# Three more matmul steps by seven products in a fused attention and MLP layer: pair 6 of two output groups, pair 1 of one down pass

## The chip, the cores and the metric

The kernel runs on one core of a Trainium2 chip. The metric is the device time of one execution in microseconds (us), as the median of several runs. The profile is one execution, recorded by the hardware profiler.

## The reference

One layer of a streaming encoder on 256 tokens (T) with width 2048 (D), all in float32, and a final norm. The part that matters here:

```python
h = x
h = h + _gla_mixer(_rmsnorm(h, gla_norm), w_in, ..., w_out)   # ends in (o * silu(r)) @ w_out
h = h + _sq_relu_mlp(_rmsnorm(h, mlp_norm), w_up, w_down)     # relu(h @ w_up)**2 @ w_down, hidden width 8192
return _rmsnorm(h, final_norm)
```

`w_out` is 2048 x 2048, `w_up` 2048 x 8192, `w_down` 8192 x 2048. Each weight is read once from HBM.

## The kernel before, in words

**Precision.** TensorE multiplies in a shortened float32 form (fp32r). A float32 product is made of three: high part by high part, high by low, low by high. So each weight tile goes through three steps after its load lands in a `raw` buffer: ScalarE casts it (`copy_hi`, L123: `hi<-raw`), VectorE subtracts (L136: `lo<-raw,hi`), and then TensorE multiplies, 256 columns at a time.

**A step by sums.** The code takes weights in pairs of channel tiles (`kp`: two tiles of 128 rows by 512 columns). A plain step over a pair takes 24 matmuls of 256 columns. A step by sums treats the pair as a 2 x 2 block product and makes it of seven block products in place of eight (a Strassen-like scheme), so 21 matmuls. They come in two halves. The first half (9 matmuls) uses three of the four blocks as they are. For the second half (12 matmuls, issued one step later, called `pending` in the code), the blocks are replaced by sums of blocks. Beside the matmuls, a step by sums differs from a plain one in this:

- The load comes as two halves of 256 KB (L334 in the output groups) in place of one of 512 KB (L337).
- POOL sends one more DMA that adds a block from HBM on top of the raw tile (L335, `accum_op=ALU.add`, 128 KB; in the down passes L1233). It must follow the first half's landing. SyncE sends all plain loads.
- ScalarE casts 768 columns for the first half, and 512 + 512 of the sums for the second (all L123).
- VectorE makes the low part of the 768 columns (L136), the weight sums L233 (256 columns, which waits for the accumulate) and L234 (512), and later the low part of the sums (1024: L365 in the output groups, L1293 in the down passes).
- The raw buffer is held until that last low part. For a plain step it is free after L136.
- The products go to four accumulators: two that hold the result blocks (B32 and BX4 in the down passes), and two that hold mixed products (P16 and P57), which are folded in at the end of a group.

On the activation side such a pair needs its tile in eight forms rather than four (sums of its blocks, `form_sums`).

**The raw buffers.** There are six (`raw_tile`, a tile pool). A new tile gets the buffer that is released first in the program's order, and its load waits for the release. The loads go out on SyncE's queue in order, so a load that waits holds back those behind it.

**The output groups** (`out_group`, `group`). `w_out` is taken in four groups of 512 columns, each over all eight pairs. The later three use the order of pairs 1, 3, 7, 2, 0, 6, 4, 5 (`ORDER[1]`). By sums are pairs 0, 1, 6, 7 in the first and the fourth group, 0, 1, 7 in the second and third. Four steps ((1, 1), (2, 1), (3, 1) and (3, 6) as group and pair) have their sums made earlier and read back from HBM. At the end of a group, `combine` folds the mixed products (two copies on ScalarE, then L926 to L929 on VectorE), and `put` (L934, one for each half of the tokens) adds that to the accumulators and writes the group's 512 columns of `h`. In the next group, after its third step (pair 7), `turn` transposes those columns on TensorE (L845), scales them (ScalarE L858, VectorE L859), for use as input to the MLP.

**The MLP** (`up`, `down`). Eight rounds m of 1024 hidden channels. Up steps and down steps alternate, step by step; the up steps run ahead, so that the end of the last rounds' down passes runs without any up step between. A pass (m, g) multiplies the round's four pairs (kp 0 to 3) of `w_down` into output group g. A fresh pass gets its accumulators one by one: `begin` copies the saved content of an accumulator into a free PSUM bank (ScalarE L1150), after `settle` has copied the last pass's content of that accumulator home and freed its bank. Mixed accumulators are begun where the first step by sums of the pass is (`first`). The last round has only passes (7, 0) and (7, 1) in this form; the second half of the columns of this round is done in the last stage by rows of `w_down` (L181), followed by the final norm. In the last round, pairs 2 and 3 of pass (7, 0) and pair 2 of pass (7, 1) are by sums.

**The order of instructions** is set by a scheduler on top of the program's order, with constraints (`issue_after`) that keep casts and low parts of the weights in sequence.

Of the kernel before, what the change touches and what calls it, by code (L numbers as in the profile page):

```python
# [69 lines left out]
def tile_gla_mlp(ctx, tc, x, xt, cols, w_vg, w_in, w_gate, w_out, w_up, w_down, final_norm, out):  # L70
# [755 lines left out]
    FORMED = (0, 1, 6, 7)  # L826
# [12 lines left out]
    def turn(src, row, gain, q, forms_of=None, banks=None):  # L839

        bs = banks or [aux_bank(), aux_bank()]
        for i in range(4):
            kt, b, o = 4 * q + i, bs[i // 2], i % 2 * T
            for t in range(NT):
                newest[0] = nc.tensor.matmul(  # L845
                    b[:, o + t * P : o + (t + 1) * P], src[:, t, kt * P : (kt + 1) * P], ident, is_transpose=True,
                    start=i % 2 == t == 0, stop=i % 2 == t == 1, skip_group_check=True,
                ).ins
        for kp in (2 * q, 2 * q + 1):
            if forms_of and kp in FORMED:  # L850
                turn_pair(kp, bs[kp - 2 * q], gain, forms_of(kp))
                continue
            for kt in (2 * kp, 2 * kp + 1):
                i = kt - 4 * q
                b, o = bs[i // 2], i % 2 * T
                s = b[:, o : o + T].rearrange("p (t s) -> p t s", t=NT)
                dh, dl = row(kt)
                nc.scalar.activation(dh, s, AF.Copy, scale=gain(kt))  # L858
                nc.vector.scalar_tensor_tensor(dl, s, gain(kt), dh.bitcast(F32), op0=ALU.mult, op1=ALU.subtract)  # L859
# [7 lines left out]
    def forms_o(kp):  # L867
        if kp < 2:
            return [of_pairs[:, kp, i] for i in range(2)]
        c = (12 * T + OFF + 128, OFF)[kp - 6]  # L870
        return [in_forms(a[:, c : c + G]) for a in (oth, otl)]
# [24 lines left out]
    def begin_out(g):  # L896

        for t in range(NT):
            out_banks[g, t] = bank = psum_bank(out_ids[2 * (g % 2) + t])
            nc.scalar.copy(bank, h[:, t, g * GT : (g + 1) * GT])  # L900
# [19 lines left out]
    def out_group(g, order, summed, between):  # L920

        def combine(p16, p57):
            tt = nc.vector.tensor_tensor
            nc.scalar.copy(comb[:, 1:3], two(p16))
            nc.scalar.copy(comb[:, 0:4:3], two(p57))
            tt(comb[:, 2], comb[:, 1], comb[:, 2], op=ALU.add)  # L926
            tt(comb[:, 0], comb[:, 0], comb[:, 2], op=ALU.subtract)
            tt(comb[:, 4], comb[:, 0], comb[:, 3], op=ALU.subtract)
            tt(comb[:, 5], comb[:, 2], comb[:, 3], op=ALU.add)  # L929

        def put(banks):
            for t in range(NT):
                o = h[:, t, g * GT : (g + 1) * GT].rearrange("p (f s) -> p f s", f=2)
                nc.vector.tensor_tensor(o, two(banks[t]), comb[:, 4 * t : 4 * t + 2], op=ALU.add)  # L934

        def at_of(kp):
            f = forms_o(kp)
            return lambda k: [a[:, k] for a in f]

        group(  # L940
            lambda kp: w_out[2 * kp * P : 2 * (kp + 1) * P, g * GT : (g + 1) * GT], [out_banks[g, t] for t in range(NT)], out_ids[4:],
            order, summed, between, row_o, at_of, combine, put, ready_of=lambda kp: made.get((None, g, kp)),
        )

    def ssq_h(g):
        for t in range(NT):
            sq = tmp.tile([P, GT], F32, tag="t512", name="sq", bufs=1)
            nc.scalar.activation(sq, h[:, t, g * GT : (g + 1) * GT], AF.Square, accum_out=hs[:, t, g : g + 1])

    ORDER = (3, 0, 2, 1, 4, 7, 6, 5), (1, 3, 7, 2, 0, 6, 4, 5)  # L950
# [6 lines left out]
    hth, htl = (big.tile([P, KT, T], F32R, tag="A" + i, name="h" + i, bufs=1) for i in "hl")  # L957
    turned_h = lambda kt: [a[:, kt, :].rearrange("p (t s) -> p t s", t=NT) for a in (hth, htl)]
    for g in range(1, GROUPS):
        out_group(g, ORDER[1], FORMED if g == 3 else (0, 1, 7), {  # L960
            2: lambda: turn(h, turned_h, g2, g - 1), 4: lambda: ssq_h(g - 1),
            **({3: lambda: begin_out(g + 1)} if g + 1 < GROUPS else {}),
        })
# [38 lines left out]
    def order_of(m):  # L1002

        return range(GROUPS)[:: 1 if m % 2 else -1]

    def by_sums(m, g, kp):

        if m == ROUNDS - 1:
            return (g, kp) in ((0, 2), (0, 3), (1, 2))
        return m < ROUNDS - 2 or g != order_of(m)[-1] or kp in (1, 2)  # L1010


# [105 lines left out]

    form = form.rearrange("p (f s) -> p f s", f=8)
    ways_of = lambda m, kp: {by_sums(m, g, kp) for g in range(GROUPS)}  # L1120

    def forms(m, kp, s):
# [64 lines left out]
    def down(passes):  # L1187
# [7 lines left out]
        for n, (m, g) in enumerate(passes):  # L1195
            fresh = not n or passes[n - 1][1] != g
            if fresh:
# [3 lines left out]
                if m == ROUNDS - 1:  # L1201
                    flush()
            ends = n + 1 == len(passes) or passes[n + 1][1] != g
            first = min(kp for kp in range(KP) if by_sums(m, g, kp)) if fresh else None

            if fresh:
                quick = first == 0
            for kp in range(KP):
                last = ends and kp == KP - 1
                alone = units + LEAD >= UPS  # L1210
                by_parts = by_sums(m, g, kp)

                def products(n, these, w, banks=banks, last=last):
# [261 lines left out]
```

## Time and profile before

| | us |
|---|---|
| median of 3 runs | 1039.96 |
| lowest, highest | 1039.46, 1041.04 |
| profiled execution | 1040.18 |
| its span, first to last instruction | 1038.4 |

| Engine | busy, us | instructions |
|---|---|---|
| TensorE (PE) | 1030.1 | 9013 |
| VectorE (DVE) | 907.3 | 1260 |
| ScalarE (ACT) | 756.0 | 1134 |
| POOL | 136.2 | 182 |

How to read the views. A row of the timeline has a start (us from the span's start), a duration, the engine, the line in the kernel, the operation, `out<-in` by the program's names, the shapes, and a count where several follow one another. What stands in brackets is idle time of the engine before the row and what ended it. `PE` is TensorE, `DVE` VectorE, `ACT` ScalarE, `SPq` SyncE's queue of DMAs. A row of a group view has the count, then the busy time and the mean duration in ns, then idle time and its releasers. A row of DMA issues has the count, the size of one, and the time from its issue to its landing in us. A row of the windows has the stretch, the sum of busy time, TensorE's busy time with its matmuls, the granted clock as a share of the full clock, the DMA share and GB/s.

### The profile page before, as it was taken

Reading aid. Unit: us, or ns where it says so; the run is one execution under the profiler, and the core shown is the slowest. Engines: PE = TensorE matmul, PEld = TensorE weight load, DVE = VectorE, ACT = ScalarE, POOL = GpSimd, SP = SyncE. Lnnn points to the kernel's source line nnn. Section 1 sums busy time; section 2 is a strip of 40 time slices with the busy share of each in tenths; the row PEclk is TensorE's granted clock in tenths of the full one; section 3 lists DMA queues with packets and bytes.
Section 4 is the critical chain, followed back from the end, with each engine's and each line's share of the span. In section 5 each row is a group of like instructions: output and inputs, shape, how many; then the busy total and the mean of one; then the engine's idle time right before and its main releaser. Section 6 shows DMA issues by size and latency. Waiting matters only on the chain.

```text
span 1038.4 us, 23392 instructions
## 1 busy us (share of the span) xinstructions
PE 1030.1 (99%) x9013; PEld 1029.5 (99%) x9013; DVE 907.3 (87%) x1260; ACT 756.0 (73%) x1134; POOL 136.2 (13%) x182
## 2 busy tenths in 40 slices
PE   9999999999999999999999999999999999999997
PEld 9999999999999999999999999999999999999997
DVE  7769769898698776989999999999999999999987
ACT  7775556676477665678779788778788778878785
POOL 0000101310100001111111111111111111111100
PEclk9999999999999999999999999999999999999999
DMA  9967868858878787678888888887888888887872
GB/s 343 332 191 212 268 186 236 211 152 308 255 230 257 242 259 198 184 208 238 231 238 228 229 235 228 236 237 224 247 228 220 250 228 229 235 237 216 239 242 91
DMA packets 128911, 240.30 MB, mean 231 GB/s; under 512 B 11504, under 2 KB 30320, under 8 KB 128672
## 3 DMA queue, kind: packets, MB, share of 16 engines
q1 hardware_dynamic: 107488, 215.32, 65.6%
q0 software_dynamic: 20592, 21.90, 12.4%
q8 instruction: 70, 1.15, 0.4%
q10 hardware_dynamic: 720, 1.60, 0.4%
q14 instruction: 41, 0.34, 0.1%
HBM read 232.48 MB, written 6.29 MB: 230 GB/s over the span
## 4 chain that ended last, share of the span: by engine, by line
PE 97%; DMA 1%; issue 1%; DVE 1%; ACT 0%; POOL 0%; POOLq 0%; DVEq 0%
PE up L1023 34%; PE acc L1023 28%; PE acc L305 15%; PE acc L181 10%; PE acc L224 6%; PE aux L224 2%; PE aux L845 1%; PE aux L696 1%; PE aux L181 1%; DMA raw<-in_w_in 0%; DMA colt<-in_cols 0%; ACT hi L123 0%; ACT sqf L1362 0%; DVE lo L136 0%; DVE comb L745 0%
## 5 line engine op out<-in xcount | busy, mean ns | idle before, releaser
L123 ACT CAST hi<-raw 128x512 fp32r<-128x512 f32 (+4 forms) x658 | 519.8, 820 | 197.9 <-DVE raw L233 66.1
L136 DVE TENSOR_TENSOR lo<-raw,hi 128x768 fp32r<-128x768 f32 (+4 forms) x228 | 233.0, 1031 | 52.9 <-ACT hi L123 49.0
L1023 PE MATMUL acc<-hi,act 128*128 128x256 f32 x1694 | 247.6, 276 | 0.0
L1023 PE MATMUL up<-hh,hi 128*128 128x256 f32 x1024 | 238.7, 276 | 0.0
L1023 PE MATMUL up<-hl,hi 128*128 128x256 f32 x1024 | 238.7, 276 | 0.0
L1023 PEld LDWEIGHTS acc<-hi,act 128*128 128x128 f32 x1694 | 217.4, 188 | 0.0
L170 DVE TENSOR_TENSOR lo<-raw,hi 128x1024 fp32r<-128x1024 f32 x160 | 194.5, 1219 | 21.5 <-ACT hi L123 18.6
L1023 PEld LDWEIGHTS up<-hl,hi 128*128 128x128 f32 x1024 | 192.3, 188 | 0.0
L1023 PEld LDWEIGHTS up<-hh,hi 128*128 128x128 f32 x1024 | 192.3, 188 | 0.0
L1233 POOL DMA_DIRECT2D raw<-in_w_down x113 | 96.9, 857 | 517.3 <-DMA raw<-in_w_down 263.2
L1293 DVE TENSOR_TENSOR lo<-raw,hi 128x1024 fp32r<-128x1024 f32 x113 | 137.7, 1218 | 1.1 <-ACT hi L123 1.1
L1023 PE MATMUL up<-hh,lo 128*128 128x256 f32 x1024 | 137.0, 276 | 0.0
L1023 PE MATMUL acc<-lo,act 128*128 128x256 f32 x847 | 133.9, 276 | 0.0
L1023 PEld LDWEIGHTS up<-hh,lo 128*128 128x128 f32 x1024 | 125.7, 188 | 0.0
L1023 PEld LDWEIGHTS acc<-lo,act 128*128 128x128 f32 x847 | 113.3, 188 | 0.0
L234 DVE TENSOR_TENSOR raw<-raw 128x512 f32<-128x512 f32 x139 | 95.9, 690 | 3.4
L233 DVE TENSOR_TENSOR raw<-raw 128x256 f32<-128x256 f32 x139 | 58.7, 423 | 11.6 <-DMA raw<-in_w_out 8.1
L181 PE MATMUL acc<-hi,xA 128*128 128x256 f32 (+1 forms) x376 | 55.6, 280 | 0.4 <-ACT hi L123 0.4
L181 PEld LDWEIGHTS acc<-hi,xA 128*128 128x128 f32 x376 | 49.5, 189 | 0.7 <-ACT hi L123 0.7
L224 PE MATMUL acc<-xA,hi 128*128 128x256 f32 x288 | 49.2, 276 | 0.0
L1150 ACT COPY sums<-acc 128x512 f32<-128x512 f32 x46 | 26.9, 585 | 22.8 <-PE acc L1023 22.7
L224 PEld LDWEIGHTS acc<-xA,hi 128*128 128x128 f32 x288 | 43.3, 188 | 0.0
(226 smaller groups left out, 1445.8 us busy)
## 6 DMA issues: line engine op xcount, KB each, us to landing
raw<-in_w_up SPq DMA_DIRECT2D x128, 512.0 KB, 4.6
raw<-in_w_down SPq DMA_DIRECT2D x226, 256.0 KB, 4.4
raw<-in_w_in SPq DMA_DIRECT2D x68, 512.0 KB, 4.9
raw<-in_w_down POOLq DMA_DIRECT2D x113, 128.0 KB, 5.1
raw<-in_w_out SPq DMA_DIRECT2D x22, 512.0 KB, 6.6
raw<-in_w_down SPq DMA_DIRECT2D x15, 512.0 KB, 5.5
raw<-in_w_vg SPq DMA_DIRECT2D x14, 520.0 KB, 8.4
raw<-in_w_in SPq DMA_DIRECT2D x24, 256.0 KB, 5.0
```

The source lines that it names most:

```text
L123: last_hi[0] = nc.scalar.copy(to, raw)
L136: last_lo[0] = nc.vector.tensor_tensor(lo[:, s], raw[:, s], hi[:, s].bitcast(F32), op=ALU.subtract)
L170: last_lo[0] = nc.vector.tensor_tensor(to[1], dst, to[0].bitcast(F32), op=ALU.subtract)
L181: newest[0] = nc.tensor.matmul(o[:, m], x, w[:, m], start=first and c == 0, stop=last, skip_group_check=True).ins
L224: nc.tensor.matmul(o, u[:, i, s], m, start=kt == 0 and n == 0 and j % 2 == 0, stop=kt == KT - 1 and n == 2, skip_group_check=True,)
L233: nc.vector.tensor_tensor(u[:, 2], u[:, 0], u[:, 2], op=ALU.subtract)
L234: return nc.vector.tensor_tensor(u[:, 1::2], u[:, 1::2], u[:, 2:3].to_broadcast([P, 2, T]), op=ALU.subtract)
L305: newest[0] = nc.tensor.matmul(bank[:, o + d : o + d + T], x, w[:, d : d + T], start=(not filled or bank in sums_banks) and bank.name not ...
L1023: newest[0] = nc.tensor.matmul(o, x, w, start=first, stop=last, skip_group_check=True).ins
L1150: last_end[0] = nc.scalar.copy(to, src).ins
L1233: nc.gpsimd.dma_start(out=raw[:, :T], in_=src[:, 0, T:], accum_op=ALU.add)
L1293: last_lo[0] = nc.vector.tensor_tensor(to[1][:, :G], u, to[0][:, :G].bitcast(F32), op=ALU.subtract)
```

## The change

Pair 6 goes by sums in the second and third output group (g = 1 and 2) too, and pair 1 of the pass (7, 1) as well.

```diff
     for g in range(1, GROUPS):
-        out_group(g, ORDER[1], FORMED if g == 3 else (0, 1, 7), {
+        out_group(g, ORDER[1], FORMED, {
             2: lambda: turn(h, turned_h, g2, g - 1), 4: lambda: ssq_h(g - 1),
...
     def by_sums(m, g, kp):
 
         if m == ROUNDS - 1:
-            return (g, kp) in ((0, 2), (0, 3), (1, 2))
+            return (g, kp) in ((0, 2), (0, 3), (1, 1), (1, 2))
         return m < ROUNDS - 2 or g != order_of(m)[-1] or kp in (1, 2)
```

`FORMED` is (0, 1, 6, 7). The eight forms of the activations for pair 6 are made before already, since the first and fourth group use them. Those of the last round's pair 1 are new: three VectorE instructions (`form_sums`), and a cast (L1135) and a low part (L1136) of 1024 columns in place of 512. In the pass (7, 1) `first` becomes 1. POOL sends three accumulates more, 12 in place of 10 for `w_out` and 114 in place of 113 for `w_down`.

As a pair by sums holds its raw buffer longer, the buffers are handed on in another order. Pair 7 of the third group had the buffer of the second group's pair 6, free after its L136; now it has that of pair 0, free after its L365. Pair 2 of the third group now has that of pair 4, and pair 0 that of pair 6 (after its L365). In the fourth group pair 7 has the buffer of the third group's pair 7 (after its L365; before, that of pair 6 after its L136).

The last combine of a group now follows the second half of pair 6 rather than that of pair 0.

On VectorE, around the end of the second output group and the third group's first steps. Here L136 of 768 columns and L233, L234 belong to pair 7 of the third group; L926 to L929 and L934 end the second group. Before:

```order
L136 TENSOR_TENSOR lo<-raw,hi 128x768
L926 TENSOR_TENSOR some<-some 128x256
L233 TENSOR_TENSOR raw<-raw 128x256
L927 TENSOR_TENSOR some<-some 128x256
L929 TENSOR_TENSOR some<-some 128x256
L234 TENSOR_TENSOR raw<-raw 128x2x256
L928 TENSOR_TENSOR some<-some 128x256
L136 TENSOR_TENSOR lo<-raw,hi 128x1024
L934 TENSOR_TENSOR h<-acc,some 128x512 x2
L365 TENSOR_TENSOR lo<-raw,hi 128x1024
```

And now:

```order
L136 TENSOR_TENSOR lo<-raw,hi 128x768
L233 TENSOR_TENSOR raw<-raw 128x256
L136 TENSOR_TENSOR lo<-raw,hi 128x1024
L234 TENSOR_TENSOR raw<-raw 128x2x256
L926 TENSOR_TENSOR some<-some 128x256
L927 TENSOR_TENSOR some<-some 128x256
L929 TENSOR_TENSOR some<-some 128x256
L365 TENSOR_TENSOR lo<-raw,hi 128x1024
L928 TENSOR_TENSOR some<-some 128x256
L934 TENSOR_TENSOR h<-acc,some 128x512
L136 TENSOR_TENSOR lo<-raw,hi 128x768
L934 TENSOR_TENSOR h<-acc,some 128x512
```

All four combines stand behind L233 now, and the L365 of pair 7 stands ahead of both L934, with the 768 columns of pair 0 between them.

On ScalarE, in the pass (7, 1), the difference of the two orders. The first two L1150 take P16 home and bring it back for this pass, the next two P57.

```order
-L123 CAST hi<-raw 128x1024
-L123 CAST hi<-raw 128x768
-L1150 COPY sums<-acc 128x512
-L1150 COPY acc<-sums 128x512
-L123 CAST hi<-raw 128x1024
+L123 CAST hi<-raw 128x768
+L1150 COPY sums<-acc 128x512
+L1150 COPY acc<-sums 128x512
+L123 CAST hi<-raw 128x768
+L1150 COPY sums<-acc 128x2x256
+L1150 COPY acc<-sums 128x512
+L123 CAST hi<-raw 128x2x256 x2
```

Before, the casts of pairs 1 and 2 stood ahead of P16's copies, and pair 3's cast between P16 and P57. Now P16 follows pair 1's cast at once, pair 2's cast stands between the copies, and the casts of pair 1's sums follow P57.

## The prediction

> **What bounds the kernel now.** I read the page first: engines, clock, chain.
>
> ```profile
> PE 1030.1 (99%) x9013; PEld 1029.5 (99%) x9013; DVE 907.3 (87%) x1260; ACT 756.0 (73%) x1134; POOL 136.2 (13%) x182
> ...
> PEclk9999999999999999999999999999999999999999
> ...
> PE 97%; DMA 1%; issue 1%; DVE 1%; ACT 0%; POOL 0%; POOLq 0%; DVEq 0%
> ```
>
> TensorE is busy 99% of the span and makes 97% of the chain, at a full granted clock. So a matmul removed is worth its pitch, and any wait that TensorE doesn't have now is paid in full. The timeline and the windows by engine give the pitch, the one pause near the change, and what followed it (start, duration, what; for the windows, TensorE's busy time and matmuls).
>
> ```profile
> 301.61 1.22 DVE L136 TENSOR_TENSOR lo<-raw,hi 128x1024 fp32r<-128x1024 f32 x1
> 302.97 0.41 PE L305 MATMUL acc<-lo,oth 128*128 128x256 f32 x2
> 304.00:312.00 8.00, 8.00 (x70) 1.00 1.01 299
> 318.00:326.00 8.00, 8.00 (x73) 1.00 0.82 267
> ```
>
> A low part came about 20 ns late (301.61 + 1.22 = 302.83) at 302.97. Afterwards 8 us held 70 matmuls, though the window is full; later, past the transposes at 313.12, they held 73. Some two of each count are cut by the window's edges, so that is about 118 ns a matmul against 113: TensorE keeps a slower pace after a pause until a specially laid step (the odd-placed tile `kp in even`, or the transposes) comes by. I take 0.1134 us for one matmul, and 4.1% for the slow pace.
>
> **The change part by part.** I sum against the profiled execution (1040.18: span 1038.4 and 1.8 around it), which stands 0.22 above the median 1039.96 of the runs. Each new step by sums drops 3 of 24 matmuls: 3 x 3 x 0.1134 = **1.02 us less**, 0.34 a step. That is the whole gain. The costs lie in three places.
>
> *Second and third output group.* The rows are VectorE's order, TensorE's transposes of a finished group (L845), SyncE's loads, and the times from a load's or an accumulate's issue to its landing (the last two rows are POOL's accumulates by the group code, of the output groups and of the whole kernel).
>
> ```profile
> 312.44 0.68 DVE L934 TENSOR_TENSOR h<-acc,some 128x512 f32<-128x512 f32 x1
> 313.12 1.03 PE L845 MATMUL aux<-ident,h 128*128 128x128 f32 x8
> 317.74 1.22 DVE L365 TENSOR_TENSOR lo<-raw,hi 128x1024 fp32r<-128x1024 f32 x1
> 318.87 3.22 DVE L136 TENSOR_TENSOR lo<-raw,hi 128x1024 fp32r<-128x1024 f32 x3
> 322.79 0.62 PE L305 MATMUL acc<-lo,of 128*128 128x256 f32 x4
> 329.11 0.43 DVE L233 TENSOR_TENSOR raw<-raw 128x256 f32<-128x256 f32 x1 [3.75 <-DMA raw<-in_w_out]
> 332.20 1.28 DVE L934 TENSOR_TENSOR h<-acc,some 128x512 f32<-128x512 f32 x2
> 334.81 1.04 PE L845 MATMUL aux<-ident,h 128*128 128x128 f32 x8
> 356.51 1.03 PE L845 MATMUL aux<-ident,h 128*128 128x128 f32 x8
> ...
> 304.00 2.37 SPq L337 DMA_DIRECT2D raw<-in_w_out  x3
> 315.15 0.81 SPq L334 DMA_DIRECT2D raw<-in_w_out  x2
> ...
> raw<-in_w_out SPq DMA_DIRECT2D x1, 512.0 KB, 7.6
> raw<-in_w_out SPq DMA_DIRECT2D x1, 256.0 KB, 3.5
> raw<-in_w_out SPq DMA_DIRECT2D x16, 256.0 KB, 5.3
> raw<-in_w_out POOLq DMA_DIRECT2D x6, 128.0 KB, 7.5
> DMA to landing us min/median/max: 5.0/7.5/7.7
> ...
> DMA to landing us min/median/max: 3.1/5.7/7.7
> ```
>
> The group views give a price for each kind of VectorE work (last: mean ns).
>
> ```profile
> L136 DVE TENSOR_TENSOR lo<-raw,hi 128x1024 fp32r<-128x1024 f32 x16 | 19.3, 1221 | 2.7 <-ACT hi L123 2.7
> L136 DVE TENSOR_TENSOR lo<-raw,hi 128x768 fp32r<-128x768 f32 x13 | 12.4, 951 | 0.0
> L234 DVE TENSOR_TENSOR raw<-raw 128x512 f32<-128x512 f32 x9 | 6.2, 687 | 0.1
> L859 DVE SCALAR_TENSOR_TENSOR hl<-aux,colt,hh 128x256 fp32r<-128x256 f32 x12 | 5.2, 478 | 0.3 <-ACT hh L858 0.3
> L926 DVE TENSOR_TENSOR some<-some 128x256 f32<-128x256 f32 x4 | 1.7, 418 | 0.0
> ```
>
> Queued instructions follow one another 0.085 earlier than their durations (318.87: 1.22 + 1.22 + 0.95 = 3.39 took 3.22), so I add pitches.
>
> Pair 6 of the second group: its load was the first of the three at 304.00 and landed in 7.6. Now it comes in two halves, the first landing near 311.0 (my estimate, 0.6 ahead of the whole). POOL then issues the accumulate; I take 7.0, near the median of the six here and below it because one took 5.0, so it lands at 318.0. VectorE's L233 waits for that, and behind it in order stand one L859, two L234, two L859 and the L365 of pair 0: from 318.05, 0.34 + 0.39 + 1.20 + 0.78 + 1.22 bring that L365's end to 322.0, where it was 318.95. TensorE wants its result 15 matmuls before 322.79's row, at 321.1, and pauses about 1 us.
>
> That L365 also frees the raw buffer into which SyncE loads the third group's pair 7. The buffer used to come from pair 6's L136, done just ahead of 315.15. Now the loads go out at 322.05. With 3.5 for the first half (the row of a half sent out at 320.1, the nearest in time; the median of sixteen is 5.3) and 7.0 for the accumulate it lands at 332.55, against L233 at 329.11 before. Behind this L233 there now stand, in order, L136, L234, three combines (L926, L927, L929), the L365 of pair 7, L928, the first L934, an L136 of 768 and the second L934: 0.34 + 1.13 + 0.60 + 1.00 + 1.13 + 0.33 + 0.60 + 0.87 + 0.68 = 6.7, so the second L934 ends at 339.3, not 333.48. The transposes need it (at 313.12 they began in the moment it ended); they move from 334.81 to 339.35, +4.5, in which all earlier pauses are swallowed. With the third group's own 0.34 off: **+4.2**. Bounds: with accumulates of 5.0 each (two of them in the chain, so 4.0 less), +0.2; with 3.1, the 0.68 saved stays; with 7.7 and loads of 5.3 (0.7, 0.7 and 1.8 more), +7.4.
>
> The Trainium skill speaks against this term: in "DMA: Bandwidth & Descriptors", section "Anatomy of one DMA — SWDGE (gpsimd) path", a GpSimd-issued transfer takes 2.0 us plus its bytes over 436e3 per us, an estimate of 2.3 for 128 KB; by it no group is late. This trace has 7.5 as the median of the six, and the sum goes by the trace.
>
> *Fourth group.* Its pair 7 takes the buffer of the third group's L365 for pair 7, its pair 0 that of pair 6. By the same steps (L365 4.7 later, 3.5, 7.0, 5.8) its L934 ends at 360.3; TensorE arrives at 339.45 + (356.51 - 334.81) - 0.34 = 360.8. No cost, 0.5 spare; at 7.7 each about 0.4 more.
>
> *The down pass.* Rows are ScalarE's and VectorE's around that pass, TensorE's start of the pair and of the last stage, and a cast's price.
>
> ```profile
> 960.43 0.96 DVE L136 TENSOR_TENSOR lo<-raw,hi 128x768 fp32r<-128x768 f32 x1 [0.16 <-ACT hi L123]
> ...
> 1001.66 0.59 ACT L1150 COPY sums<-acc 128x512 f32<-128x512 f32 x1 [2.74 <-PE acc L1023]
> 1002.15 0.59 ACT L1150 COPY acc<-sums 128x512 f32<-128x512 f32 x1
> 1004.61 1.15 ACT L123 CAST hi<-raw 128x512 fp32r<-128x512 f32 x2
> 1006.70 1.08 ACT L1150 COPY h<-acc 128x512 f32<-128x512 f32 x2
> ...
> 1001.69 0.50 PE L1023 MATMUL acc<-hi,act 128*128 128x256 f32 x3
> 1009.51 0.73 PE L181 MATMUL acc<-hi,act 128*128 128x256 f32 x5
> ...
> L123 ACT CAST hi<-raw 128x768 fp32r<-128x768 f32 x13 | 10.9, 838 | 0.2
> ```
>
> The forms of pair 1's activations grow (three L1128, L1136 and L1135 doubled): three pitches of 0.34 and the 0.54 that a width of 1024 takes more than one of 512, 1.6 us of VectorE near 955. They are hidden: by 960.43 VectorE is waiting for ScalarE again. Without that cover they would cost those 1.6 once.
>
> In the pass itself the bank P16 is free at 1001.66 and back at 1002.74. Before, 24 plain matmuls of pair 1 covered that. Now pair 1 has only its six B32 matmuls (to 1002.37), waits for P16, and ends at 1003.19. The cast of pair 2 ends at 1003.48, its low part at 1004.6: first half of pair 2 done at 1004.94. P57's two copies end at 1004.48, the two casts of pair 1's sums at 1005.55, their low part at 1006.8: TensorE waits again, second half done at 1007.4. Pair 3's cast stands behind two copies home (1.0 together) and ends at 1007.5; pair 3 runs 1007.6 to 1010.3 and pair 2's second half to 1011.7. The last stage starts at 1011.7, not at 1009.51: **+2.2** with its 0.34 off. At the slow pace, these 36 matmuls cost 0.2 and the 19.6 us of the last stage, which has no specially laid step, 0.8: **+3.2**. Bounds: 2.2 without the pace, 0 if the copies come earlier than I put them.
>
> Sum: 4.2 + 3.2 = 7.4 (the 1.02 included): 1047.6 against the profiled run, **1047.4** on the median.
>
> **The rivals.**
>
> *Quick accumulates (0.15).* If they land in 5.0, the groups cost 0.2 and the pass stays at 3.2: 1043.4. One of six did so; the median of 7.5 speaks against it.
>
> *The pass is covered (0.11).* If ScalarE has the casts before P16 is asked for, only the groups are late: 4.2 - 0.34, or 1043.8. For it: 2.74 of idle time before 1001.66. Against: that idle time ends with TensorE's release of P16 and can't be moved forward.
>
> *The clock drops after a long pause (0.12).* TensorE would stand about 3.1 us at the third group's transposes. Here it started with this row:
>
> ```profile
> 0.78 3.75 PE L399 MATMUL aux<-const-float32-1.0 128*128 128x128 f32 x16 [0.78 <-PEq L1464]
> ```
>
> That is 0.234 each, where eight transposes of that width take 1.04; 16 would have taken under 2. A restart like that costs about 2: 1049.4. Against: no pause in this trace dropped PEclk. The Trainium skill has this rule ("TensorE: Matmul & The Clock Gate", section "HAM oscillation — how this bites in real kernels"): no idle gap of TensorE over some 3.4 us, or it falls back to the slow clock. No pause of this trace within the work is long enough to show it.
>
> *Not slower (0.16).* One mechanism: the accumulates land as the quickest of the kernel do, in 3.1, since they meet no other load in their queues. Then L233 is on time, pair 0's L365 too, and the groups keep their 0.68; with the pass at +2.2 that is 1041.5, and with the pass covered 1038.9, the whole 1.02 below the median. It decides if the third group's L233 starts by 327.7 and P16 is back by 1002.4. For it: the overall median is 5.7, not 7.5. Against: w_out's own six. That the change removes no matmuls I exclude: the order shows 21 in place of 24 in the three steps.
>
> **How the numbers follow.** My main case has 0.46. Some 0.2% of the time, 2.1 us, is what a measurement of this kernel can tell from no change. Below 1041.5 lies part of the last rival, above 1051 (7.7 each, loads of 5.3 and the slow pace) the clock together with late groups: the range is 1041.5 to 1051.0. Only 1.02 is taken out, so a gain of 2.1 us needs something unseen: of the last rival 0.02 goes to faster and 0.14 to no change; all else is slower, 0.84.
>
> **What would show it.** Right: an idle VectorE ahead of L233 near 332, the third group's transposes at about 339, a pause of some 3 us ahead of them; ScalarE's L1150 pair at 1002 to 1004 (shifted by 4.2) with TensorE waiting for pair 1's casts; and 118 ns pitch in the last stage. Wrong: the transposes within 1 us of 334.5, accumulates landing in under 5, or a last stage starting 1.4 us or less after its old distance from pair 1.

## The result, and the profile after

| | before | changed |
|---|---|---|
| median of 6 runs, us | 1040.02 | 1045.51 |
| lowest, highest | 1039.46, 1041.86 | 1044.44, 1048.85 |
| ratio, 95% interval | | 1.0057 [1.0043, 1.0071] |
| profiled execution (span) | 1040.18 (1038.4) | 1048.85 (1047.1) |

The changed kernel is 5.5 us slower. Its six times fall in two heaps, 1044.4 to 1046.4 and 1048.6 to 1048.9, and so do the six of a repetition below. The profiled execution belongs to the upper heap, so the profile shows the cost in an execution of that heap, 8.7 us.

The page's first part: TensorE has 9 matmuls fewer, and 5 us more of busy time.

```profile
PE 1035.2 (99%) x9004; PEld 1032.7 (99%) x9004; DVE 913.8 (87%) x1272; ACT 759.8 (73%) x1140; POOL 140.6 (13%) x185
```

The timeline around the second and third output group, for VectorE, SyncE and TensorE:

```profile
316.96 0.42 DVE L233 TENSOR_TENSOR raw<-raw 128x256 f32<-128x256 f32 x1 [0.96 <-DMA raw<-in_w_out]
...
319.69 1.22 DVE L365 TENSOR_TENSOR lo<-raw,hi 128x1024 fp32r<-128x1024 f32 x1
...
331.38 0.42 DVE L233 TENSOR_TENSOR raw<-raw 128x256 f32<-128x256 f32 x1 [4.20 <-DMA raw<-in_w_out]
...
336.14 0.68 DVE L934 TENSOR_TENSOR h<-acc,some 128x512 f32<-128x512 f32 x1
...
337.61 0.68 DVE L934 TENSOR_TENSOR h<-acc,some 128x512 f32<-128x512 f32 x1
...
320.93 0.81 SPq L334 DMA_DIRECT2D raw<-in_w_out  x2
...
336.88 0.44 PE L845 MATMUL aux<-ident,h 128*128 128x128 f32 x2 [1.18 <-DVE h L934]
338.34 1.54 PE L845 MATMUL aux<-ident,h 128*128 128x128 f32 x6 [1.03 <-DVE h L934]
...
361.66 1.03 PE L845 MATMUL aux<-ident,h 128*128 128x128 f32 x8
```

This is the forecast chain, link by link, some 1 us ahead of the forecast times. L233 of pair 6 waits for its accumulate to 316.96 (forecast 318.05). The L365 of pair 0 ends at 320.91 (322.0), and in the same moment SyncE sends the third group's pair 7 (before: 315.15). Its accumulate holds L233 to 331.38 (332.6). The second write of h ends at 338.29 (339.3; before: 333.48). The transposes begin at 336.88 and end behind it (before, they began at 334.81). TensorE pauses twice, with two transposes between. The pause of about 1 us that the forecast had ahead of these, for pair 0's low part, did not come.

What the forecast's main case lacks stands in the windows behind that place (TensorE's busy time and matmuls; the next column is the granted clock):

```profile
335.00:338.00 3.00, 1.14 (x8) 1.00 0.43 114
338.00:341.00 3.00, 2.66 (x13) 0.50 1.03 334
341.00:344.00 3.00, 3.00 (x26) 0.93 0.45 165
344.00:352.00 8.00, 8.00 (x70) 1.00 0.80 236
```

From 337.98 on the clock is at one half for 3.41 us. In 338 to 341 there are 13 matmuls, where the kernel before had 29:

```profile
338.00:341.00 3.00, 3.00 (x29) 1.00 0.99 382
```

Then 70 matmuls in 8 us show the slow pace up to the next transposes.

The down pass, ScalarE and then TensorE:

```profile
1006.82 0.59 ACT L1150 COPY sums<-acc 128x512 f32<-128x512 f32 x1 [3.06 <-PE acc L1023]
1007.30 0.59 ACT L1150 COPY acc<-sums 128x512 f32<-128x512 f32 x1
...
1007.95 0.50 PE L1023 MATMUL acc<-hi,act 128*128 128x256 f32 x2 [0.26 <-ACT acc L1150]
...
1012.02 0.74 PE L1023 MATMUL acc<-lo,act 128*128 128x256 f32 x4 [0.53 <-DVE lo L1293]
...
1017.02 0.99 PE L181 MATMUL acc<-hi,act 128*128 128x256 f32 x7
1018.00:1026.00 8.00, 8.00 (x71) 1.00 0.34 124
```

TensorE waits for P16's copy and for the low part of pair 1's sums, as forecast, and the last stage has 71 matmuls in 8 us (before, 73).

All profiles of this study can be laid side by side by four marks, which are starts of TensorE's rows: the first transpose of the turn in the second, the third and the fourth output group, the first matmul of the last stage (L181) and the last matmul of all. The stages between them repeat within 0.02 wherever nothing disturbs them, while the time up to the first mark differs by up to 2.4 between executions (312.0 to 314.4), and that from the last mark to the end of the span by up to 1.2 (7.25 to 8.41). So a gain of 0.3 to 0.7 that the marks show can be lost in a single total. In us:

| kernel | second to third turn | third to fourth | fourth to L181 | L181 to the last |
|---|---|---|---|---|
| before | 21.69 | 21.70 | 653.00 | 21.65 |
| changed | 23.64 | 24.78 | 655.36 | 22.49 |
| repeated | 23.34 | 23.93 | 655.35 | 22.50 |
| groups only | 24.38 | 24.91 | 652.99 | 21.65 |
| second group only | 24.33 | 26.39 | 653.01 | 21.64 |
| third group only | 21.69 | 21.36 | 653.00 | 21.65 |
| pass only | 21.69 | 21.70 | 655.36 | 22.49 |
| buffer of its own | 21.35 | 21.35 | 653.01 | 21.64 |
| sum on VectorE | 21.62 | 21.35 | 653.00 | 21.65 |
| idle transposes | 24.01 | 21.72 | 655.35 | 22.50 |
| long pause | 24.89 | 23.34 | 652.99 | 21.65 |

Where a turn has its pause within its eight transposes, a part of the pause and the slow clock count to the next column. The changed kernel's sums against before: groups 48.42 less 43.39, +5.0; pass 655.36 + 22.49 less 653.00 + 21.65, +3.2.

### The profile page after: what moved, and what is told of

It is laid out like the page before. It is cut to its first block, busy times and chain, and to the rows that moved or that the text cites. A ratio compares the mean times of both kernels' runs of the same rounds, so it can differ in the third digit from the quotient of the medians.

```text
span 1047.1 us, 23410 instructions
## 1 busy us (share of the span) xinstructions
PE 1035.2 (99%) x9004; PEld 1032.7 (99%) x9004; DVE 913.8 (87%) x1272; ACT 759.8 (73%) x1140; POOL 140.6 (13%) x185
## 5 line engine op out<-in xcount | busy, mean ns | idle before, releaser
L136 DVE TENSOR_TENSOR lo<-raw,hi 128x768 fp32r<-128x768 f32 (+4 forms) x228 | 232.6, 1028 | 55.3 <-ACT hi L123 51.0
L234 DVE TENSOR_TENSOR raw<-raw 128x512 f32<-128x512 f32 x142 | 97.8, 690 | 3.4
L233 DVE TENSOR_TENSOR raw<-raw 128x256 f32<-128x256 f32 x142 | 59.9, 423 | 9.1 <-DMA raw<-in_w_out 5.2
L181 PE MATMUL acc<-hi,xA 128*128 128x256 f32 (+1 forms) x376 | 56.4, 283 | 0.1
L181 PEld LDWEIGHTS acc<-hi,xA 128*128 128x128 f32 x376 | 50.0, 191 | 0.5 <-ACT hi L123 0.4
L1150 ACT COPY sums<-acc 128x512 f32<-128x512 f32 x46 | 26.9, 584 | 22.7 <-PE acc L1023 22.6
```

The costliest lines, as they stand in the source:

```text
L136: last_lo[0] = nc.vector.tensor_tensor(lo[:, s], raw[:, s], hi[:, s].bitcast(F32), op=ALU.subtract)
L181: newest[0] = nc.tensor.matmul(o[:, m], x, w[:, m], start=first and c == 0, stop=last, skip_group_check=True).ins
L233: nc.vector.tensor_tensor(u[:, 2], u[:, 0], u[:, 2], op=ALU.subtract)
L234: return nc.vector.tensor_tensor(u[:, 1::2], u[:, 1::2], u[:, 2:3].to_broadcast([P, 2, T]), op=ALU.subtract)
L1150: last_end[0] = nc.scalar.copy(to, src).ins
```

## The experiments

Each first line is the kernel's edit; "as before" or "as changed" names what it starts from. Ratios are to runs of the kernel before on the same chip, with the 95% interval.

**The changed kernel again.**

> The changed kernel once more, for a second profile and more times. Both theories: between 1044.4 and 1048.9, as before. If the spread of its times is the clock, a profile of a time near 1044.5 shows the granted clock at 1.00 around the third output group's transposes, where the first profile has 0.50 for 3.1 us; if it is the accumulates, its transposes begin earlier than 338.3.

Measured: median 1048.35, ratio 1.0070 [1.0058, 1.0083]; 1044.6, 1045.96, and four of 1048.28 to 1048.93. The mean granted clock of the span was 0.998 in the two short ones and 0.996 to 0.997 in the four long ones. In the first six runs it was the same: 0.997 in the two above 1048, 0.998 in the four below. So the two heaps go with the mean clock in all twelve. That mean also counts the end of the span, where TensorE has no work left and the clock is at one half for 2.1 to 5.6 us in the fourteen traces of this study. By this, 0.996 needs a drop elsewhere and 0.998 leaves no room for one of 3.4 us, while 0.997 can come with or without one (the profile of the sum on VectorE, below, has 0.997 and no other drop). The profile fell in the upper heap again, with the same drop:

```profile
338.00:341.00 3.00, 2.14 (x10) 0.54 0.94 282
```

No profile shows an execution of the lower heap.

**The output groups alone.** As changed, without pair 1 of the pass.

```diff
-            return (g, kp) in ((0, 2), (0, 3), (1, 1), (1, 2))
+            return (g, kp) in ((0, 2), (0, 3), (1, 2))
```

> Only the two steps of the output groups. Theory (late hand-over of a raw buffer delays the third group's transposes, the down pass costs a fixed 3.2): 1.2 to 5.2 slower than before, the rest of the change's cost less 3.2; transposes at about 338, last stage at 113 ns a matmul. Rival (the down pass costs little, all comes from the groups): 5 or more slower.

Measured: 1044.82 (1041.12 to 1046.60), 1.0041 [1.0026, 1.0057]. The late third turn comes with the groups, and so does a wide scatter. The last stage has its old pace: 73 matmuls in 1018 to 1026.

```profile
312.38 1.04 PE L845 MATMUL aux<-ident,h 128*128 128x128 f32 x8
336.76 0.44 PE L845 MATMUL aux<-ident,h 128*128 128x128 f32 x2 [1.59 <-DVE h L934]
338.23 0.89 PE L845 MATMUL aux<-ident,h 128*128 128x128 f32 x6 [1.03 <-DVE h L934]
...
1018.00:1026.00 8.00, 8.00 (x73) 1.00 0.04 14
```

**The pass alone.** As before, with pair 1 of the pass (7, 1) (the diff's second part only).

> Only the step in the last down pass. Theory: the last stage starts 2.2 later, its matmuls take 118 ns in place of 113, together 3.2 slower (1043.2), with next to no scatter. Rival (covered by ScalarE's idle time): 0.3 faster to 0.5 slower.

Measured: 1043.82 (1042.88 to 1046.74), 1.0040 [1.0028, 1.0052]. The profile has +2.36 up to the last stage and +0.84 in it, 3.2 in all. The scatter is larger than expected.

```profile
1002.25 0.50 PE L1023 MATMUL acc<-hi,act 128*128 128x256 f32 x2 [0.26 <-ACT acc L1150]
...
1006.32 0.74 PE L1023 MATMUL acc<-lo,act 128*128 128x256 f32 x4 [0.53 <-DVE lo L1293]
...
1018.00:1026.00 8.00, 8.00 (x70) 1.00 0.01 2
```

**The second group's pair 6 alone.** As before.

```diff
-        out_group(g, ORDER[1], FORMED if g == 3 else (0, 1, 7), {
+        out_group(g, ORDER[1], FORMED if g != 2 else (0, 1, 7), {
```

> Only pair 6 of the second output group. Theory (its accumulate delays pair 0's low part, which frees the buffer of the third group's pair 7): the same as with both groups, 0.34 more. Rival (the third group's own step makes the cost, as POOL's accumulates queue there): 0.3 faster to 0.5 slower.

Measured: 1047.49 (1045.86 to 1048.26), 1.0067 [1.0054, 1.0080]. One step alone costs 7.4, more than both steps together (4.7). In the profile the clock stays at one half for two windows, not one:

```profile
338.00:341.00 3.00, 2.17 (x10) 0.50 0.89 300
341.00:344.00 3.00, 3.00 (x16) 0.50 0.97 382
```

**The third group's pair 6 alone.** The same edit with `g != 1`.

> Only pair 6 of the third output group. Theory (it needs the second group's step to make a late chain; the fourth group has 0.5 to spare): third group's transposes where they were before, fourth group's 0.34 earlier or up to 1 later, 0.4 faster to 1 slower. Rival (each of the two steps is late on its own): 3 to 5 slower.

Measured: 1040.55 (1040.10 to 1042.95), 1.0007 [0.9998, 1.0016], no difference that can be told. The turns are at 312.57, 334.26 and 355.62: 21.69 as before, then 21.36, the step's 0.34 less. So this step alone is covered, and it is the second group's that makes the third turn late.

**A buffer of its own for the third group's pair 7.** The groups alone, and:

```diff
-            raw = raw_tile()[:, : 2 * GT]
+            raw = wpool.tile([P, G], F32, tag="more", name="raw", bufs=1) if kp in own else raw_tile()[:, : 2 * GT]
...
-            order, summed, between, row_o, at_of, combine, put, ready_of=lambda kp: made.get((None, g, kp)),
+            order, summed, between, row_o, at_of, combine, put, ready_of=lambda kp: made.get((None, g, kp)), own=(7,) if g == 2 else (),
```

> Only the two steps of the output groups, and the third group's pair 7 has a raw buffer of its own (one that the program uses only later), so its load needs not wait for pair 0's low part of sums. Theory (the buffer's hand-over is the link): its accumulate is issued before 322 and lands by 329, L233 is on time, VectorE's order alone may still cost 0 to 1: between 0.7 faster and 1 slower. Rival (the accumulates are late by themselves, or the order of VectorE): 2 to 5 slower as with the two steps alone.

Measured: 1040.10 (1039.37 to 1043.00), 1.0006 [0.9997, 1.0015]; by the profile both groups gain their 0.34 in full. The extra buffer stood empty from the start, so the load went out at 36.07 already and the accumulate at 43.60: not only the hand-over is gone, but the wait for this accumulate too. L233 finds its accumulate landed, VectorE's order is still the new one, and TensorE has no pause:

```profile
326.23 0.42 DVE L233 TENSOR_TENSOR raw<-raw 128x256 f32<-128x256 f32 x1
...
332.44 0.69 DVE L934 TENSOR_TENSOR h<-acc,some 128x512 f32<-128x512 f32 x1
...
312.63 1.03 PE L845 MATMUL aux<-ident,h 128*128 128x128 f32 x8
333.98 1.03 PE L845 MATMUL aux<-ident,h 128*128 128x128 f32 x8
355.33 1.03 PE L845 MATMUL aux<-ident,h 128*128 128x128 f32 x8
```

With the load and its accumulate out of the way the cost is gone. The new order of VectorE's rows costs nothing as long as L233 is on time.

**The sum on VectorE in place of the accumulate.** The groups alone, and in the groups two to four for pairs 6 and 7:

```diff
-                nc.gpsimd.dma_start(out=raw[:, :T], in_=src[:, 0, T:], accum_op=ALU.add)
+                if kp not in added:
+                    nc.gpsimd.dma_start(out=raw[:, :T], in_=src[:, 0, T:], accum_op=ALU.add)
...
+                        if kp in added:
+                            tt(u[:, 0], u[:, 0], u[:, 1], op=ALU.add)
                         weight_sums(u)
```

> Only the two steps of the output groups, and in groups two to four VectorE adds the block that POOL's accumulate brought for pairs 6 and 7 (it lies in the same raw tile), one instruction of 256 columns (0.34) each. Theory (the wait for the accumulates, twice in one chain, is what moved the transposes): no pause, no clock drop, transposes at 334.5 less or equal, 0.7 faster than before (0 to 1). Rival (VectorE's new order, both writes of the group behind the low parts, or the buffer held until the low part of the sums): still 2 or more slower.

Measured: 1040.24 (1039.26 to 1042.27), 1.0007 [0.9998, 1.0016]. The turns are 21.62 and 21.35 apart (21.62 holds a stretch of slow pace from 330.4 on). The buffers are handed on as in the changed kernel, the load of the third group's pair 7 goes out at 321.15, and yet there is no late transpose: the late hand-over alone doesn't make the cost. But VectorE's order is another one too. Both writes of h stand ahead of pair 7's low part of sums and of the 768 columns of pair 0, as in the kernel before (L350 is the sum that replaces the accumulate, L937 the write):

```profile
327.33 0.42 DVE L350 TENSOR_TENSOR raw<-raw 128x256 f32<-128x256 f32 x1
...
331.33 0.42 DVE L233 TENSOR_TENSOR raw<-raw 128x256 f32<-128x256 f32 x1
...
333.28 1.28 DVE L937 TENSOR_TENSOR h<-acc,some 128x512 f32<-128x512 f32 x2
```

L233 is no earlier than in the changed kernel (331.38), but from its start to the end of the writes there are 3.2 us, not 6.9. So this run takes away the accumulates and the order behind L233 together, and it can't tell which of the two was needed. The gain of 0.7 that was expected isn't to be told from none.

**Idle transposes in the pause.** As changed, and in the third group:

```diff
+        for _ in range(fill):
+            newest[0] = nc.tensor.matmul(bs[0][:, :P], ident, ident, is_transpose=True, start=True, stop=True, skip_group_check=True).ins
         for i in range(4):
...
-            2: lambda: turn(h, turned_h, g2, g - 1), 4: lambda: ssq_h(g - 1),
+            2: lambda: turn(h, turned_h, g2, g - 1, fill=20 * (g == 2)), 4: lambda: ssq_h(g - 1),
```

> The whole change, and 20 idle transposes of the identity on TensorE just ahead of the third group's transposes, which write what the real ones overwrite. They take about 2.2 us of the pause and delay nothing by more than 0.5. Theory (the upper cluster of times, near 1048.5, is the clock gate answering to the pause): granted clock 1.00 there, all times near 1044 to 1046, none at 1048. Rival (the two clusters come from the accumulates, the clock drop is a symptom): still times at 1048 in about half the runs.

Measured: 1047.20 (1046.03 to 1047.28), 1.0067 [1.0054, 1.0081]. The clock stays whole, and no time lies above 1047.3:

```profile
335.00:338.00 3.00, 3.00 (x29) 1.00 0.97 224
338.00:341.00 3.00, 2.86 (x25) 1.00 0.92 320
```

So the drop is an answer to TensorE's idleness. What it costs together with the slow pace can be read by comparing this profile with the changed kernel's: the second write of h starts at the same time (337.69, there 337.61), and the fourth group's turn begins 1.9 earlier (359.73, there 361.66). But no time is near 1044.5 either. A part of this lies outside the program: a time is here 2.0 to 2.6 above its span, in all other kernels 1.7 to 1.9. The spans, 1043.9 to 1045.2, stand between those of the lower heap (1042.7 to 1044.6) and the upper (1046.5 to 1047.2), nearer to the lower. So the drop and the pace explain about half of the 4 us between the heaps. The other half stays open; that the filling holds up the transposes where the writes of h come earlier is possible, and not shown.

**A pause by itself, short and long.** As before, with one or two idle instructions ahead of the second group's writes of h (two shown):

```diff
         def put(banks):
+            for _ in range(2 * (g == 1)):
+                nc.vector.tensor_tensor(comb, comb, comb, op=ALU.max)
```

> The kernel before, and after the second output group's combine one idle VectorE instruction of 1536 columns (the larger of a value and itself), about 1.7 us, ahead of both writes of h; the order puts a low part (1.1) there as well. TensorE then waits once, 1.5 us, at the third group's transposes. Theory (only a pause near 3 us brings the clock down; the transposes reset the pace): clock 1.00, 1.0 to 2.0 slower. Rival (any pause at this place costs 4 and more): 4 slower.

> The same with two such instructions, and two low parts between: TensorE waits once, about 4.1 us. Theory (the clock gate): granted clock 0.50 for 3 to 7 us behind it, so 1.5 to 3.5 more than the pause, 6 to 8.5 slower. Rival (a pause costs its length): 4.1 slower, clock 1.00.

Measured, short: 1040.92 (1039.45 to 1044.93), 1.0010 [1.0000, 1.0019]; long: 1045.07 (1041.23 to 1046.34), 1.0043 [1.0029, 1.0057]. The turns and the clock, of the long one first:

```profile
313.14 1.03 PE L845 MATMUL aux<-ident,h 128*128 128x128 f32 x8
338.03 2.14 PE L845 MATMUL aux<-ident,h 128*128 128x128 f32 x8 [3.04 <-DVE h L936]
...
338.00:341.00 3.00, 2.97 (x13) 0.50 0.97 378
```

```profile
314.01 1.10 PE L845 MATMUL aux<-ident,h 128*128 128x128 f32 x8
335.76 1.29 PE L845 MATMUL aux<-ident,h 128*128 128x128 f32 x8
...
338.00:341.00 3.00, 3.00 (x28) 1.00 1.00 378
```

Both pauses came out shorter than expected. In the short one TensorE came to the third group's turn 0.9 later than before, while VectorE, tied to the DMAs, was no later (its L233 at 328.94, before 329.11): a pause is the difference of these two, and TensorE's start moves it from execution to execution. What is left of the pause in this profile is about 0.2 between two transposes, so the run tests neither theory. In the long one a single pause of a little over 3 us halved the clock. It has no step by sums added, so the clock needs nothing of the change but the pause. Its 5.1 lies between the two theories' numbers, because the pause was 3.04 and not 4.1: by the marks the two stages are 4.84 longer than before, 1.8 more than the pause, within the 1.5 to 3.5 of the first theory. One of its six times is 1041.23 with a clock of 0.999.

**Pair 3 in place of pair 1 in the pass.** As before, and `(1, 3)` added in place of `(1, 1)`; the second half of the last pair runs within the last stage.

```diff
-            return (g, kp) in ((0, 2), (0, 3), (1, 2))
+            return (g, kp) in ((0, 2), (0, 3), (1, 2), (1, 3))
...
+                if n + 1 == len(passes) and pending:
+                    to_end.append(pending)
...
             held.append((kt, w))
+            while to_end:
+                for _ in to_end.pop():
+                    pass
```

> In the last down pass pair 3 goes by sums in place of pair 1 (output groups as before), its second half runs between the last stage's first matmuls. P16 then has the cover of two plain pairs as before. Theory (the pass's cost is the uncovered copy of P16 and what queues behind it, then the pace): no pause ahead of the last stage, pace 113, 0.3 faster to 0.5 slower. Rival (ScalarE has no room for one more step by sums in this pass, wherever it is): 2 or more slower.

Measured: 1042.65 (1042.36 to 1044.13), 1.0029 [1.0018, 1.0041]. P16 has its cover and there is no pause at it, but the next cast on ScalarE is late, and the slow pace follows (71 matmuls in 1018 to 1026):

```profile
1008.13 1.18 PE L181 MATMUL acc<-hi,act 128*128 128x256 f32 x7 [0.58 <-ACT hi L123]
```

The theory that P16's cover was the whole matter falls here: ScalarE's queue of copies and casts had no room for a further step at either of the two places that were tried in this pass.

**A pause in the pass by itself.** As before, and:

```diff
+                for _ in range(2 * ((m, g, kp) == (ROUNDS - 1, 1, 3))):
+                    copy_hi(raw, raw)
                 w = parts(raw, 2 * GT, slots(), [(T * by_parts, 2 * GT)])
```

> The kernel before, and two idle copies on ScalarE (raw onto itself, 0.95 each) ahead of the cast of pair 3 in the last down pass; same steps, same tiles. Pauses of TensorE of 0.2 at pair 3 and 0.8 at the last stage, 1.0 in all. Theory (a pause brings the slow pace, and nothing in the last stage resets it): 118 ns a matmul up to the end, 1.2 more, 2.2 slower. Rival (the slow pace came from where the tiles lie, not from the pause): 113 ns, 1.0 slower.

Measured: 1042.33 (1041.12 to 1043.49), 1.0019 [1.0010, 1.0028]. The total fits, the way to it doesn't. After the first pause the 16 matmuls of the first row below start 117 to 119 ns apart, and 113 ahead of it, with the same tiles in the same places: a pause does bring the slow pace. But two more pauses follow, and behind the last of them the pace is the quick one again:

```profile
1004.84 2.15 PE L1023 MATMUL acc<-hi,act 128*128 128x256 f32 x16 [0.35 <-ACT hi L123]
...
1009.84 1.18 PE L181 MATMUL acc<-hi,act 128*128 128x256 f32 x7 [0.49 <-ACT hi L123]
...
1018.00:1026.00 8.00, 8.00 (x73) 1.00 0.00 0
```

So a pause can end the slow pace as well as begin it. None of these kernels is faster than the one before by more than can be told.

## Why the prediction was right or wrong

**The saving of 0.34 a step** was right: third group only and buffer of its own show 21.36 and 21.35 in place of 21.70 wherever nothing is late.

**The chain through the raw buffer** was right: the rows of the changed kernel show each link, the second group's pair 6 makes it alone, and with pair 7's load and accumulate out of the way the cost is gone. Its times were about 1 late throughout, since the first accumulate landed at 316.9 and not at 318.0, and the 1 us of pause that it had at 321.1 was not there. The second write of h is 4.8 later than before (338.29, 333.48). Of this, 2.3 is the later L233 (331.38, 329.11) and 2.5 is VectorE's new order behind it (6.9 us up to the end of the writes, before 4.4). The prediction had both terms, as 3.4 and 2.3. The buffer of its own takes away the late L233 and keeps the order, and nothing is lost. No run takes away the order alone: the sum on VectorE changed the accumulates and the order.

**The fourth group without a wait** was right: its turn has no pause in the changed kernel. One wait was not foreseen: at 329.89 TensorE waits 0.31 for ScalarE's copy of the second group's mixed products (L924), behind which the third group gets that bank.

**The pass** was right in mechanism and size: 2.36 to the start of the last stage (forecast 2.2) and 0.84 behind it (0.8, and 0.2 within the pass), 3.2 in all (3.2).

**The clock** was the step that failed. The main case left it whole, and a drop had a chance of 0.12 as a rival, with the remark that no pause of that trace could show it. (The trace of the kernel before does have a drop, behind TensorE's last matmul; the last section reads it.) It drops in both profiles of the changed kernel, and by the mean clock in up to six of the twelve executions. It takes not one pause of 3.4 but two, 1.18 and 1.03, with two transposes between. Its direct loss is about 1.5 (3.0 us of work at half the clock). The slow pace up to the next turn, which the main case took to be reset by the transposes, adds some 0.8; here it had begun at the wait of 329.89, ahead of the turn. The rule of the Trainium skill ("TensorE: Matmul & The Clock Gate", section "HAM oscillation — how this bites in real kernels"), no idle gap over some 3.4 us, is borne out in kind by the long pause, whose row has 3.04 of idle time; as a threshold it was too generous here, where 1.18 and 1.03 of idle time were enough.

**The size** follows from these. The profiled execution is 8.7 over before: 5.0 for the groups (4.2 forecast, where the pauses were shorter than forecast and the clock and the pace made up for it), 3.2 for the pass, and some 0.4 in the start and the end of the execution. The 5.0 can be followed: counted from start to start, TensorE's three waits at 329.89, 336.88 and 338.34 took 3.0 over the pitch, the half clock 1.5, the slow pace from 330.1 on 1.0, and the two steps saved 0.7, which makes 4.8. The median of six was +5.5 and that of the repetition +8.3, on either side of the forecast +7.4, as the executions of one heap or the other had the majority. No execution lies between 1046.42 and 1048.28, where the forecast is. That it comes so close to the medians is partly luck: in the groups' term, waits put too long stood in for a loss of clock and pace that the main case left out. What makes the lower heap's executions 4 quicker, when the direct loss of clock and pace is about 2, stays open: presumably their pause is shorter, but none was recorded.

**The quick accumulates** (a rival) did not come: the eight of the changed kernel's output groups took 5.4 in the median and up to 7.4, and the two that matter about 6.7 each (issued at 310.20 and 324.54, landed at 316.87 and 331.29).

## What to carry to other kernels

A step that holds a buffer longer pays where the buffer's next owner is due, not where the step stands: look up who gets the buffer next and how long a load and all that follows it take. On an engine that is busy 99% of the time, a pause can cost more than its length, through the clock and the pace behind it. Before a step is added for 0.34 us, find the engine that hasn't that much room: here ScalarE in the last pass.

## What the runs showed of the hardware that was not expected

The clock is decided by fixed stretches of time. In all fourteen traces the granted clock changes only at whole multiples of 3.413 us from its first rise, and that rise lies anywhere from 3.75 to 6.89 us after the start. So each execution has a grid of such stretches, in another place relative to the work. In the changed kernel the clock fell at 337.98, and in the stretch that ended there TensorE had been busy for 46%: the two pauses of 1.2 and 1.0 us counted together, though 0.4 of work lies between them. In the five traces with a drop in the third group, the stretch ahead of it was busy for 15 to 46%. At the end of the kernels, where TensorE runs out of work, a last stretch that was busy for 7 to 43% brought the drop at once (nine traces), and one that was busy for 53 to 78% did not (five traces; in the kernel before 57% up to 1032.90, then nothing, and the drop at 1036.32). By these traces the line lies between 46% and 53%. The drop lasted one stretch in four of the five and two in the second group alone, where the first slow stretch was busy for 72%; 82% and more brought the clock back. Twenty idle transposes in the gap kept it at 1.00.

With the two pauses of the changed kernel, about half of the possible places of the grid put half a stretch of idle time (1.7 us) into one stretch; this is an estimate from their rows. It fits a drop in about half of the executions, but no execution without one was recorded, so it isn't shown that the grid decides.

The slow pace of 118 ns a matmul in place of 113 is a state that a pause may begin or end. In the five traces with a drop in the third group, the pace behind it was the one that stood ahead of the pause: slow in the changed kernel, in the groups alone and in the second group alone, where it had begun between 320 and 331 (70 matmuls in 8 us in the first two), and quick in the repetition and in the long pause by itself. A turn at the full clock did end the slow pace, in the kernel before at 313 and with the sum on VectorE at 336. In the pass with the two idle copies it ended at a third pause (429 ns from one start to the next, at 1011.10); with pair 3 by sums, a pause of 424 ns at the same matmul left it slow. What decides isn't shown.
